# A hybrid Mamba-2 and short-convolution decoder layer on one core: y of four chunks kept in SBUF, a 128-row second product for the samples, and a new written order of the engines

## The chip, the cores and the metric

The kernel runs on one core of one Trainium2 chip. Its time is the device time of one execution in microseconds, as the median of several runs. The core has five engines that each take their own instructions in order: TensorE (PE; PEld is its weight load), VectorE (DVE), ScalarE (ACT), GpSimd (POOL) and SyncE (SP), which issues nearly all of the DMAs here. An engine whose next instruction waits for another engine or for a DMA holds everything that stands behind that instruction.

## What is computed

One decoder layer in float32 over a prompt of 1024 tokens, with 16 learned meta tokens ahead of it, and over 8 samples of 8 tokens that carry states. Cut to what matters here:

```python
proj = rmsnorm(h, norm_mix_pre) @ w_in         # gate_b, gate_c, hv, z, xbc, dt
u = gate_c * hv                                # short convolution, 512 wide
conv_u, new_buf_sc = causal_dwconv(u, buf_sc, sconv_w)
ya = group_rmsnorm(gate_b * conv_u, sconv_norm, 8)
xs, Bm, Cm = split(silu(causal_dwconv(xbc, buf_xbc, ssm_conv_w) + ssm_conv_b))
y, s = ssd_chunked(xs, dt, A, Bm, Cm, s, 128)  # 16 heads of 64, state 128
y = (y + D_skip * xs) * silu(z)
yb = group_rmsnorm(y, ssm_norm, 2)
h = h + rmsnorm(concat(ya, yb) @ w_out, norm_mix_post)
fn = rmsnorm(h, norm_ffn_pre)
h = h + rmsnorm((silu(fn @ w_gate) * (fn @ w_up)) @ w_down, norm_ffn_post)
```

The outputs are the rows of the prompt and of the samples and the new states of both convolutions and of the SSD recurrence.

## The kernel before

All products keep float32's accuracy by splitting an operand in a high and a low part of PE's faster type (fp32r): a projection is three products, high by high, high by low and low by high (`xh`, `xl` and `whi`, `wlo` in L398; `mhb`, `mlb` and `woh`, `wol` in L1192). The tokens are cut in chunks of 128, one to eight; 0 is the meta tokens and 9 the samples.

The work runs through these stages: the projections of x, B and C (`px`, to about 180 us); the projection of z (`pz`) and then the three of the short convolution (`pc`, `ph`, `pb`, each in groups 0 to 3 of 128 channels and token tiles 0 to 2, which are 256, 320 and 512 wide), to about 530 us, and among them the SSD passes of the chunks and the states of the samples; the output projection (`o`, three groups of chunks, L1192), to about 675 us; and the feed-forward part.

An SSD pass of chunk i (`ssd_chunk`, L859) makes y of the chunk (`y_of`, L702: the products `po` with the state and `pd` with the masked matrix M, L750, added on DVE up to L754) and the next state (`st`, L786; `S`, L873 and L875 on DVE). y_of stores y in the DRAM array d_y (L757). Later `finish(i)` (L759) loads it in a tile `yf` (two buffers, L761) and z in `zt`, multiplies (L766), forms the sums of squares (L768 to L772: `zt`, `sg`), takes them over the partitions by a product with ones (`pn`, L774), the root (L775) and the reciprocal (L776), scales (L779) and stores the result in d_yb (L780). FIN says after which chunk's pass which chunks are finished.

The short convolution's `sconv_out` (L836) multiplies a projection `pb` into `gc` (L840), squares it (L844), sums over groups by the product `sn` (L846), and takes the root (L847), the reciprocal (L850) and the product (L851); then the row goes to d_ya (L852).

A sample state (`sample_state`, L905; u from 0 to 7) takes the outer products of B and x of four samples by two products into one bank: `b1` holds B's high part in its upper and in its lower 64 rows, `xs2` the high part of x in rows 0 to 63 and the low part in rows 64 to 127, and so L938 gives high by high and high by low. `b2` holds B's low part in 64 rows, and L939 multiplies it by the upper 64 rows of xs2. Two such pairs make a state, and b1 and b2 are built on DVE for every second state.

Where the passes end, `final_state` (L972) transposes the last state S8 (`fsp`, L975), copies it on ACT (`fso`, L977) and stores it (L978). `slp` (L1010) and `slo` (L1012) do the same for the last rows of the convolution. The operands of the output projection come through `load_mix` (L1120): SP loads a chunk's finished rows (`mrb` from d_yb, L1126, two buffers; `mra` from d_ya), ACT makes the high part (`mhb`, L1133) and DVE the low one (`mlb`, L274). The weights come as `wo` (L1178), `woh` (ACT, L1181) and `wol` (DVE, L1182). A chunk's first four products need mhb, the fifth and sixth mlb.

The order of all this is not left to the program's text. ISSUE (L56) holds, for each of the five engines, the order of its instructions as numbered runs, and the code near L1620 puts each engine's instructions in that order.

Of the kernel before, what the change touches and what calls it, by code (L numbers as in the profile page):

```python
# [8 lines left out]
F32 = mybir.dt.float32  # L9
F32R = mybir.dt.float32r  # L10
# [6 lines left out]
P = 128  # L17
# [20 lines left out]
YB = 1  # L38
# [14 lines left out]
FIN = {4: (1,), 5: (2, 3, 4), 6: (5,), 7: (6,), 8: (7,), 9: (8,)}  # L53
# [179 lines left out]
def hymba_kernel(ctx, tc, x_prompt, x_sample, state_sconv, state_ssm_conv, state_ssm, meta_tokens,  # L233
# [647 lines left out]
    def samples_begin():  # L881
# [18 lines left out]
        E, y = y_of(i, xb, bt, xd, None)  # L900
        return xs2, bt, cs, E, y

    bms = {}

    def sample_state(u, st):  # L905

# [750 lines left out]
```

## Time and profile before

| | |
|---|---|
| median of three runs | 1387.33 us (1385.71, 1387.34, 1387.33) |
| the profiled execution | 1386.58 us |
| its span, first to last instruction | 1384.9 us |
| granted TensorE clock | 0.998 |
| DMA | 240.51 MB, mean 174 GB/s |

The page gives busy times of the engines over the span, a strip of 40 slices with tenths of busy time and of the granted clock, the chain of waits that ended last, and groups of instructions by line. A timeline's rows are start and duration in microseconds, the engine, the line, the operation, what it writes and reads, the shape and how many rows are taken together; a value in brackets is the time that the engine stood still ahead of it. PE's products overlap, so what a product costs PE is the distance to the next start. In a table of stretches the figures after the stretch's length are the busy times of PE, PEld, DVE, ACT and POOL, then the granted clock, the share of the DMA engines in use and GB/s. A row that begins with a line and ends in "| busy, mean" is a group of equal instructions.

### The profile page before, as it was taken

The numbers are of one execution on the slowest core, as the hardware profiler recorded it, in microseconds if no ns is written. First come the engines' busy times: TensorE is split into PE (matmuls) and PEld (weight loads), VectorE is DVE, ScalarE is ACT, GpSimd is POOL, SyncE is SP. The second block draws the span as 40 slices with busy tenths as digits, with TensorE's granted clock in tenths as the row PEclk, the third lists the DMA queues.
The fourth block names the chain that finished last, engine by engine and source line by source line (L and its number), as shares of the span: only waits on it lengthen the run. The fifth ranks groups of instructions, "written<-read, shape, count | busy, mean of one in ns | idle before, by whom it ended". The sixth has DMA issues, their size and how long they took to land.

```text
span 1384.9 us, 22044 instructions
## 1 busy us (share of the span) xinstructions
PE 1366.9 (99%) x8841; PEld 1228.5 (89%) x8841; DVE 976.9 (71%) x1332; ACT 585.9 (42%) x948; POOL 52.1 (4%) x106
## 2 busy tenths in 40 slices
PE   7999999999999999999999999999999999999997
PEld 6889998888898888887899999999999998888886
DVE  6555457878898988677599876766666766455565
ACT  6466445443364354556663233222232234344431
POOL 2000000000000000001100000000000000000001
PEclk9999999999999999999999999999999999999999
DMA  6136347778755457765445644344443379655543
GB/s 216 48 106 154 95 109 200 214 188 222 203 158 173 130 188 258 246 217 195 156 136 182 235 163 161 110 153 169 146 148 129 126 246 331 209 180 169 179 164 134
DMA packets 212543, 240.51 MB, mean 174 GB/s; under 512 B 33421, under 2 KB 161505, under 8 KB 212442
## 3 DMA queue, kind: packets, MB, share of 16 engines
q1 hardware_dynamic: 212442, 239.12, 54.6%
q8 instruction: 69, 1.13, 0.3%
q14 instruction: 32, 0.26, 0.1%
HBM read 170.29 MB, written 68.79 MB: 173 GB/s over the span
## 4 chain that ended last, share of the span: by engine, by line
PE 91%; DVE 4%; DMA 2%; ACT 1%; issue 1%; SPq 0%; POOL 0%; DVEq 0%; POOLq 0%; ACTq 0%
PE d L1580 15%; PE px L398 11%; PE o L1192 9%; PE pz L398 7%; PE yg L1237 6%; PE yu L1237 6%; PE xg L1237 4%; PE xu L1237 4%; PE zu L1237 4%; PE zg L1237 4%; PE pc L398 3%; PE pb L398 3%; PE ph L398 3%; PE pd L750 1%; PE st L786 1%
## 5 line engine op out<-in xcount | busy, mean ns | idle before, releaser
L398 PE MATMUL px<-xh,whi 128*128 128x272 f32 (+2 forms) x288 | 94.8, 337 | 0.0
L398 PE MATMUL px<-xl,whi 128*128 128x272 f32 (+2 forms) x288 | 93.7, 333 | 0.0
L398 PE MATMUL px<-xh,wlo 128*128 128x272 f32 (+2 forms) x288 | 93.3, 332 | 0.0
L274 DVE TENSOR_TENSOR wlo<-raw,whi 128x1024 fp32r<-128x1024 f32 x32 | 39.0, 1218 | 47.3 <-ACT whi L282 47.3
L1182 DVE SCALAR_TENSOR_TENSOR wol<-wo,vec,woh 128x1024 fp32r<-128x1024 f32 x36 | 46.0, 1279 | 34.7 <-ACT woh L1181 34.5
L398 PE MATMUL pz<-xh,whi 128*128 128x256 f32 (+2 forms) x192 | 64.6, 337 | 0.0
L1181 ACT ACTIVATE woh<-wo,vec 128x1024 fp32r<-128x1024 f32 x36 | 41.4, 1149 | 53.6 <-PE o L1192 42.5
L398 PE MATMUL pz<-xh,wlo 128*128 128x256 f32 (+2 forms) x192 | 63.9, 333 | 0.0
L398 PE MATMUL pz<-xl,whi 128*128 128x256 f32 (+2 forms) x192 | 63.7, 332 | 0.0
L430 DVE SCALAR_TENSOR_TENSOR xa<-xr,vec,xa 128x1128 f32<-128x1128 f32 x36 | 50.1, 1392 | 11.9 <-ACT xa L427 11.0
L398 PEld LDWEIGHTS px<-xh,whi 128*128 128x128 f32 x288 | 54.6, 193 | 4.3
L398 PEld LDWEIGHTS px<-xl,whi 128*128 128x128 f32 x288 | 54.0, 190 | 4.2 <-issue 0.2
L398 PEld LDWEIGHTS px<-xh,wlo 128*128 128x128 f32 x288 | 54.0, 190 | 3.7
L1580 PE MATMUL d<-wd,B01h 128*128 128x512 f32 x176 | 54.2, 389 | 0.0
L282 ACT ACTIVATE whi<-raw 128x1024 fp32r<-128x1024 f32 x32 | 33.8, 1055 | 38.4 <-PE px L398 18.2
L1580 PE MATMUL d<-wd,T3h 128*128 128x512 f32 x152 | 46.8, 389 | 0.0
L1192 PE MATMUL o<-wol,mhb 128*128 128x512 f32 x144 | 44.4, 394 | 0.0
L1580 PE MATMUL d<-wd,T2h 128*128 128x512 f32 x144 | 44.2, 389 | 0.0
L1580 PE MATMUL d<-wd,B11h 128*128 128x512 f32 x144 | 44.2, 389 | 0.0
L1192 PE MATMUL o<-woh,mhb 128*128 128x512 f32 x144 | 39.3, 397 | 1.3 <-ACT woh L1181 1.0
L1192 PE MATMUL o<-woh,mlb 128*128 128x512 f32 x128 | 40.3, 392 | 0.0
L398 PEld LDWEIGHTS pz<-xh,whi 128*128 128x128 f32 x192 | 36.1, 188 | 3.9 <-issue 1.3
(694 smaller groups left out, 4062.4 us busy)
## 6 DMA issues: line engine op xcount, KB each, us to landing
wo<-in_w_out_dram SPq DMA_DIRECT2D x36, 512.0 KB
raw<-in_w_in_dram SPq DMA_DIRECT2D x32, 512.0 KB
wg<-in_w_gate_dram SPq DMA_DIRECT2D x11, 1024.0 KB
wu<-in_w_up_dram SPq DMA_DIRECT2D x11, 1024.0 KB
xr<-in_w_down_dram SPq DMA_DIRECT2D x11, 1024.0 KB
d_t<-xr SPq DMA_DIRECT2D x11, 1024.0 KB
xt<-in_x_prompt_dram SPq DMA_DIRECT2D x16, 512.0 KB
M<-d_a SPq DMA_DIRECT2D x16, 512.0 KB
```

The source lines that it names most:

```text
L274: V.tensor_tensor(out=out, in0=a, in1=hi.bitcast(F32), op=ALU.subtract)
L282: S.activation(hi[:, :], raw[:, :], AF.Copy)
L398: PE.matmul(acc, (hi, lo, hi)[q][:, wk], (xh, xh, xl)[q][t][:, k, o:], start=n_ == 0, stop=n_ + 1 == len(order))
L430: V.scalar_tensor_tensor(out=dst, in0=part(row, i), scalar=wv[:, wcol(i):wcol(i) + 1], in1=dst, op0=ALU.mult, op1=ALU.add)
L750: PE.matmul(pdv[64 * e:64 * e + 64, h // 2, :w], xd[:w, h * 64:(h + 1) * 64], Ms[h // 8][:w, h % 8, :w], start=True, stop=True)
L786: PE.matmul(st[:, g * 512:(g + 1) * 512], bt[:w, g * P:(g + 1) * P], xw[:w, g * 512:(g + 1) * 512], start=True, stop=True)
L1181: S.activation(hi, raw, AF.Copy, scale=nv)
L1182: V.scalar_tensor_tensor(out=lo, in0=raw, scalar=nv, in1=hi[:, :].bitcast(F32), op0=ALU.mult, op1=ALU.subtract)
L1192: PE.matmul(accs[i][c], l[:, kb, :], r_[:, c * 512:(c + 1) * 512], start=n == 0 and q == 0, stop=n == 11 and q == len(steps) - 1)
L1237: PE.matmul(acc[:, c, 0:W1], w_[l][k], b[r_][:, k, c * W1:(c + 1) * W1], start=start and k == 0 and x == 0, stop=k == 3 and x == 2, skip_g ...
L1580: PE.matmul(accs[t], sx[x][:, tl], wx[y], start=st and x + y == 0, stop=en and x == 1, skip_group_check=n not in OPENS)
```

## The change

There are three parts.

First, y of chunks 4 to 7 stays in SBUF: the tile of y has two buffers instead of one (YB), y_of keeps it and finish works in it, so four stores to d_y and four loads from it go; yf of the other chunks has one buffer. FIN finishes chunks 4 to 7 each right after its own pass, and chunks 1, 2 and 3 after those of 5, 6 and 7.

Second, b2 becomes one tile of 128 rows for all states, whose lower 64 rows are filled with zeros once; L939 multiplies it by all 128 rows of xs2.

Third, ISSUE holds another order for all five engines. Of its numbers a first row stands for all.

```diff
-YB = 1
+YB = 2
+KEPT = (4, 5, 6, 7)
...
-FIN = {4: (1,), 5: (2, 3, 4), 6: (5,), 7: (6,), 8: (7,), 9: (8,)}
+FIN = {4: (4,), 5: (5, 1), 6: (6, 2), 7: (7, 3), 9: (8,)}
...
 ISSUE = {
     "Pool": """
-0+2 3+3 2+1 6+5 15+1 11+1 17+1 12+3 16+1 18+1 20+1 19+1 22+1 21+1 24+1 23+1 26+1 25+1 28+1 27+1 32+1 31+1 30+1 29+1
+0+2 3+3 2+1 6+4 15+1 10+2 17+1 12+3 16+1 18+1 20+1 19+1 22+1 21+1 24+1 23+1 26+1 25+1 28+1 27+1 32+1 31+1 30+1 29+1
...
-        SY.dma_start(d_y[i][:, :, :], y)
+        if i in KEPT:
+            kept[i] = y
+        else:
+            SY.dma_start(d_y[i][:, :, :], y)
+
+    kept = {}
...
-        y = pf.tile([P, 8, P], F32, tag="yf", name=f"yf{i}", bufs=2)
-        SY.dma_start(y[:, :, :w], d_y[i][:, :, :])
+        if i in KEPT:
+            y = kept.pop(i)
+        else:
+            y = pf.tile([P, 8, P], F32, tag="yf", name=f"yf{i}")
+            SY.dma_start(y[:, :, :w], d_y[i][:, :, :])
...
+        b2 = po.tile([P, 4, P], F32R, tag="bm2", name="bm2")
+        V.tensor_copy(b2[w:2 * w].rearrange("p a (c n) -> p (a c) n", n=w),
+                      ident[w:2 * w, 0:w].unsqueeze(1).to_broadcast([w, 8, w]))
+        bms["lo"] = b2
...
-            b2 = po.tile([w, 4, P], F32R, tag="bm2", name=f"bm2{u}")
+            b2 = bms["lo"]
...
-            for dst, h in ((b1[0:w], 0), (b1[w:2 * w], 0), (b2, w)):
+            for dst, h in ((b1[0:w], 0), (b1[w:2 * w], 0), (b2[0:w], w)):
...
-            PE.matmul(o, xs2[0:w, xj], b2[:, :, :].rearrange("p b n -> p (b n)"), start=False, stop=True)
+            PE.matmul(o, xs2[:, xj], b2[:, :, :].rearrange("p b n -> p (b n)"), start=False, stop=True)
```

The lines of the changed kernel are numbered otherwise: L1192 is L1203 there, L274, L398, L846, L850 and L851 are L273, L397, L853, L857 and L858, and L1126, L1133 and L1182 are L1137, L1144 and L1193. The numbers behind a name are those of the tiles; o_5181 and o_5195 are the first chunk's sums of the output projection in the new and the old order, mhb_5165 and mhb_5179 its high part, and d_yb_70 to d_yb_77 are chunks 1 to 8.

The order of PE where the state passes end and the output projection begins. Before, where the transposes `fsp` stand 76 rows ahead of the first o row, and pb and `sn` of the last group are still among the o products:

```order
L398 MATMUL pb_1_5056<-xl_170,whi 128x320
L1192 MATMUL o_5195<-woh_5201,mhb_5179 128x512 x2
L1192 MATMUL o_5195<-wol_5202,mhb_5179 128x512 x2
L1192 MATMUL o_5196<-woh_5201,mhb_5185 128x512 x2
L398 MATMUL pb_2_5089<-xh_168,whi 128x512
L398 MATMUL pb_2_5089<-xh_168,wlo 128x512
L398 MATMUL pb_2_5089<-xl_171,whi 128x512
L846 MATMUL sn_5050<-sq_5048,bd_125 128x256
```

Now, with `pd` and `st` of chunk 8 a few rows ahead:

```order
L397 MATMUL pb_2_5075<-xh_168,wlo 128x512
L397 MATMUL pb_2_5075<-xl_171,whi 128x512
L986 MATMUL fsp<-ident,S_4800 128x128 x8
L853 MATMUL sn_5102<-sq_5034,bd_125 128x512
L1021 MATMUL slp<-ident,slast 18x128 x4
L781 MATMUL pn_5284<-sg_5281,ones 128x2x64
L1203 MATMUL o_5181<-woh_5187,mhb_5165 128x512 x2
L1203 MATMUL o_5181<-wol_5188,mhb_5165 128x512 x2
L1203 MATMUL o_5181<-woh_5187,mlb_5166 128x512 x2
L1203 MATMUL o_5181<-woh_5211,mhb_5165 128x512 x2
L1203 MATMUL o_5181<-wol_5212,mhb_5165 128x512 x2
```

All products of pb, which stood between fsp and the o products and among these, now stand ahead of fsp.

The order of DVE at the same place. Before, a piece from the reciprocals of the convolution's third row on (`sq_4944`) with the first two low parts mlb, which the o products read:

```order
L850 RECIPROCAL sq_4944<-sq_4944 128x256
L840 TENSOR_TENSOR gc_4220<-pb_2_4983,gc_4220 128x512
L1182 SCALAR_TENSOR_TENSOR wol_5202<-wo_5199,vec,woh_5201 128x1024
L850 RECIPROCAL sq_4944<-sq_4944 128x320
L274 TENSOR_TENSOR mlb_5180<-mrb_5177,mhb_5179 128x1024
L840 TENSOR_TENSOR gc_4618<-pb_0_5022,gc_4618 128x256
L274 TENSOR_TENSOR mlb_5186<-mrb_5183,mhb_5185 128x1024
```

Now, the row that ends the state's update (S_4800, for which fsp waits) and those behind it, and then the end of the same list with the first two low parts:

```order
L882 TENSOR_TENSOR S_4800<-st_4797,S_4800 128x1024
L847 TENSOR_TENSOR gc_4620<-pb_2_5075,gc_4620 128x512
L778 TENSOR_TENSOR zt_5277<-zt_5277 128x2x2x64
L779 TENSOR_TENSOR sg_5281<-zt_5277 128x2x64
L1193 SCALAR_TENSOR_TENSOR wol_5212<-wo_5209,vec,woh_5211 128x1024
L857 RECIPROCAL sq_5034<-sq_5034 128x160 x2
L857 RECIPROCAL sq_5034<-sq_5034 128x256
```

```order
L857 RECIPROCAL sq_4930<-sq_4930 128x256
L858 TENSOR_TENSOR gc_4209<-gc_4209,sq_4930 128x512
L858 TENSOR_TENSOR gc_4209<-gc_4209,sq_4930 128x320
L858 TENSOR_TENSOR gc_4209<-gc_4209,sq_4930 128x256
L1023 COPY slo<-slp 18x512
L273 TENSOR_TENSOR mlb_5166<-mrb_5163,mhb_5165 128x1024
L273 TENSOR_TENSOR mlb_5172<-mrb_5169,mhb_5171 128x1024
```

Between the two pieces stand the reciprocal of sg (L783), two products yf (L786), a reciprocal of sq_5034 with 256 columns and three products L858 of gc_4620. The reciprocals and products of the convolution's last two rows, gc_4209 and gc_4620, which stood among the low parts or behind them, now stand between the state's update and the first low part.

The order of SP there. Before:

```order
L757 DMA d_y_87<-y_4725 128x1024
L978 DMA out_dram<-fso 128x8x128
L1126 DMA mrb_5177<-d_yb_70 128x1024
L1126 DMA mrb_5183<-d_yb_71 128x1024
L780 DMA d_yb_76<-yf_4801 128x1024
L764 DMA zt_5420<-d_z 128x8x128
L1178 DMA wo_5305<-in_w_out_dram 128x1024
L762 DMA yf_5418<-d_y_87 128x1024
L1126 DMA mrb_5189<-d_yb_72 128x1024
L1126 DMA mrb_5377<-d_yb_73 128x1024
L1126 DMA mrb_5383<-d_yb_74 128x1024
```

Now, from the last load of zt on:

```order
L771 DMA zt_5406<-d_z 128x8x128
L1189 DMA wo_5315<-in_w_out_dram 128x1024
L989 DMA out_dram<-fso 128x8x128
L1137 DMA mrb_5163<-d_yb_70 128x1024
L1137 DMA mrb_5169<-d_yb_71 128x1024
L1088 DMA xt_5621<-in_x_prompt_dram 128x1024
L1048 DMA post_bc<-in_norm_mix_post_dram 128x1024
L1088 DMA xt_5677<-in_x_prompt_dram 128x1024
L1050 DMA ffn_bc<-in_norm_ffn_pre_dram 128x1024
```

```order
L859 DMA d_ya<-gc_4209 128x1088
L1024 DMA out_dram<-slo 16x512
L1025 DMA out_dram<-slo 2x512
L1137 DMA mrb_5175<-d_yb_72 128x1024
L1137 DMA mrb_5363<-d_yb_73 128x1024
L769 DMA yf_5404<-d_y_87 128x1024
```

The store of fso stands ahead of the first two loads mrb in both orders. Between the second and the third mrb stood four transfers; now it is nine, with the stores of two of the convolution's rows (d_ya) and of slo among them.

More of the change, by code (lines that the diff above doesn't have):

```diff
@@ L879, in hymba_kernel @@
     o_nat = o_s_s[0].rearrange("b g e p n -> b (g e p) n")
+    bms = {}
     def samples_begin():
@@ L901, in samples_begin @@
         return xs2, bt, cs, E, y
-    bms = {}
     def sample_state(u, st):
```

296 rows, old and new, of the table ISSUE are left out of this document.

## The prediction

> **What bounds the kernel now.** I read the page first, then the table of stretches for the two stages in which the change does most, and then single rows.
>
> ```profile
> span 1384.9 us, 22044 instructions
> PE 1366.9 (99%) x8841; PEld 1228.5 (89%) x8841; DVE 976.9 (71%) x1332; ACT 585.9 (42%) x948; POOL 52.1 (4%) x106
> PEclk9999999999999999999999999999999999999999
> PE 91%; DVE 4%; DMA 2%; ACT 1%; issue 1%; SPq 0%; POOL 0%; DVEq 0%; POOLq 0%; ACTq 0%
> 330.00:520.00 190.00, 190.00 (x1297) 165.38 (x1296) 168.11 (x217) 90.10 (x160) 6.18 (x10) 1.00 0.61 176
> 520.00:675.00 155.00, 153.73 (x699) 125.11 (x698) 112.82 (x127) 84.33 (x118) 11.88 (x12) 1.00 0.70 227
> ```
>
> PE is busy 99% of the span, and the chain of waits runs 91% over PE. So two things alone move the time: PE's own work, and new moments at which PE stands. In 330 to 520 us (first figure after the length: PE) PE has no gap at all, while DVE (third figure) is busy 168 of 190 us; in the output projection (520 to 675 us) PE lacks 1.3 us. There is almost nothing to win from waits, and much to lose if PE's order runs into DVE's.
>
> The executions shown have a median of 1387.33 us. The profiled one took 1386.58 us, 1.7 us more than its span; I sum against 1386.58, which lies 0.75 us below the median.
>
> **Part 1: the second product over 128 rows.** The start times in PE's timeline around the first sample state:
>
> ```profile
> 240.29 0.31 PE L398 MATMUL pz<-xl,whi 128*128 128x320 f32 x1
> 240.44 0.40 PE L938 MATMUL s1p<-bm,xs 128*128 128x512 f32 x1
> 240.76 0.49 PE L939 MATMUL s1p<-bm,xs 64*128 64x512 f32 x1
> ...
> 242.05 0.42 PE L398 MATMUL pz<-xh,whi 128*128 128x320 f32 x1
> 242.30 0.31 PE L398 MATMUL pz<-xh,wlo 128*128 128x320 f32 x1
> ...
> 244.36 0.39 PE L398 MATMUL pz<-xh,whi 128*128 128x512 f32 x1
> 244.59 0.40 PE L398 MATMUL pz<-xh,wlo 128*128 128x512 f32 x1
> L939 PE MATMUL s1p<-bm,xs x16: 492/498/502, 240.8 to 442.8; 64*128 64x512 f32 x16
> ```
>
> The second column is a product's duration; what PE pays is the distance from one start to the next. With 128 rows a 512-wide one takes 244.59 - 244.36 = 0.23 us, and a 320-wide one 240.44 - 240.29 = 0.15. The four products of a state, alternating between 128 and 64 rows, take 242.05 - 240.44 = 1.61 us, and the next product 0.25 instead of 0.15. With 128 rows throughout I expect 4 x 0.23 + 0.15 = 1.07 instead of 1.86 us: 0.79 us per state, and 16 products at L939 are 8 states, so **6.3 us less**. The bounds: nothing (if the 64-row form is not what costs), and 16 x (0.498 - 0.23) = 4.3 us plus 8 x 0.5 us for L938's share of the alternation, 8.3. I take 6.3, which these rows give directly. The copy of zeros that fills the tile's lower half once is one DVE instruction more; a small one here costs 0.3 us, and in 187 to 330 us PE never waited.
>
> [...]
>
> In the new order the products with M (L750, 64 columns of output) of chunks 6 and 8 stand in one run each instead of two. At 0.1 us for entering and 0.1 for leaving such a run (0.25 against 0.15 above) that is **0.4 us less**.
>
> **Part 2: y kept in SBUF.** Four stores and four loads of 512 KB go. In 330 to 520 us PE had no gap, so no load of y held it, and the queue's share (0.61, the last figure but one of that row) leaves room: I cost it at nothing, and no gain is possible where nothing waited. It moves the finishing of chunks 1 to 3 to the end, and so the load of DVE.
>
> **Part 3: the order at the handover** from the state passes to the output projection. Before, after the transposes of the final state:
>
> ```profile
> 506.29 1.04 PE L975 MATMUL fsp<-ident,S 128*128 128x128 f32 x8
> 520.87 0.63 PE L1192 MATMUL o<-woh,mhb 128*128 128x512 f32 x2
> 507.39 1.01 ACT L977 ACTIVATE fso<-fsp 128x1024 f32<-128x1024 f32 x1
> 508.43 0.39 SPq L978 DMA_DIRECT2D out_dram<-fso  x1
> 508.87 1.76 SPq L1126 DMA_DIRECT2D mrb<-d_yb  x2
> 519.15 8.29 SPq L1126 DMA_DIRECT2D mrb<-d_yb  x3
> L1133 ACTq EVENT_SEMAPHORE  x1: 17/17/17, 514.8 to 514.8; - x1
> L1133 ACT ACTIVATE mhb<-mrb x4: 1047/1050/1062, 515.5 to 525.1; 128x1024 fp32r<-128x1024 f32 x4
> 523.95 2.20 ACT L1133 ACTIVATE mhb<-mrb 128x1024 fp32r<-128x1024 f32 x2
> 530.75 1.53 PE L1192 MATMUL o<-woh,mhb 128*128 128x512 f32 x6
> 532.12 0.39 PE L1192 MATMUL o<-wol,mhb 128*128 128x512 f32 x1
> 532.81 1.02 PE L846 MATMUL sn<-sq,bd 128*128 128x512 f32 x2
> 533.67 0.60 PE L1010 MATMUL slp<-ident,slast 128*18 128x128 f32 x4
> 534.03 0.71 PE L1192 MATMUL o<-wol,mhb 128*128 128x512 f32 x2
> ```
>
> From fsp's end (507.3) to the first o product lay 13.5 us of pb products, and under them went fso (ACT), its store, the load of mrb1 (issued 508.87, landed by 514.8: 5.9 us) and mhb1. SP stays in order: mrb1 stands behind the store of fso, before and after. After the change the pb products all stand ahead of fsp, and between fsp and the first o product are only sn32, slp and pn9.
>
> What PE has from the end of S8 (DVE, L875, for which fsp waits) until the fifth o product, the first to read mlb1: fsp 1.0, sn32 and slp 534.03 - 532.81 = 1.2, pn9 0.3 (my estimate, as the shorter of two such small products), four o products at (532.12 - 530.75) / 6 = 0.23, 0.9: together 3.4 us. DVE's list over the same stretch is priced by its groups in 504 to 550 us (name, shape, busy time, mean ns):
>
> ```profile
> L1182 DVE SCALAR_TENSOR_TENSOR wol<-wo,vec,woh 128x1024 fp32r<-128x1024 f32 x6 | 7.6, 1262 | 0.2
> L850 DVE RECIPROCAL sq<-sq 128x256 f32<-128x256 f32 x3 | 5.1, 1728 | 0.0
> L274 DVE TENSOR_TENSOR mlb<-mrb,mhb 128x1024 fp32r<-128x1024 f32 x4 | 4.8, 1199 | 0.0
> L850 DVE RECIPROCAL sq<-sq 128x160 f32<-128x160 f32 x2 | 2.2, 1120 | 0.0
> L776 DVE RECIPROCAL sg<-sg 128x128 f32<-128x128 f32 x1 | 0.9, 944 | 0.0
> L851 DVE TENSOR_TENSOR gc<-gc,sq 128x512 f32<-128x512 f32 x2 | 1.4, 687 | 0.0
> 512.50 1.74 DVE L850 RECIPROCAL sq<-sq 128x256 f32<-128x256 f32 x1
> 514.16 0.63 DVE L840 TENSOR_TENSOR gc<-pb,gc 128x512 f32<-128x512 f32 x1
> ```
>
> Between S8 and mlb1 now stand one wol (1.26), reciprocals of 2 x 160, 3 x 256 and 128 columns (2.24 + 5.18 + 0.94) and twelve light ones, the longest 687 ns, half a microsecond in the mean (6.0); with mlb1 itself (1.20) that is 16.8 us. A row starts 0.08 us ahead of the end of the one before (512.50 + 1.74 against 514.16), so 20 rows take 1.6 us less: **mlb1 is ready 15.2 us after S8**. PE then stands 15.2 - 3.4 = **11.8 us** in two pieces: first for mhb1, which is ready after fsp 1.0, fso 1.0, an issue 0.4, the load 5.9 and mhb1 1.05, that is 9.4 us after S8, where PE has 2.5 us of work (6.9 us); then for mlb1 (15.2 - 9.4 - 0.9: 4.9 us). Behind the waiting product stands all of the output projection, so nothing of PE's passes it.
>
> A third piece: mrb3 takes mrb1's buffer, so SP issues it only when mlb1 is done, and holds yf8 and the next loads behind it (before: issued 519.15, mhb3 begun 523.95, 4.8 us). mhb3 is ready 4.8 + 1.05 = 5.9 us after mlb1, and PE has 20 products, 4.6 us, so it waits **1.3 us**. Bounds of part 3: 11 us, if DVE is 5% quicker and mrb3 lands within PE's 4.6 us; 19 us, if each load takes twice as long (mhb1 5.9 us later, which swallows the wait for mlb1 but for 0.3, and mhb3 4.8 later). I take 13.1, the nearest to these rows.
>
> Is it given back? PE lacked 1.3 us in the whole projection, so at most that much of a later wait can be absorbed, and after 675 us PE is full.
>
> **Part 4: the rest of the order.** I find one more place, pb of group 2, tile 1, whose bank DVE frees only behind a reciprocal of chunk 7 (256 columns, some 1.73 us), and a few of half a microsecond. DVE, at 168 of 190 us, has 22 us to spare, but spread. I allow **2.5 us**, between 0 and 5.
>
> **Sum**: 1386.6 - 6.3 - 0.4 + 11.8 + 1.3 + 2.5 = 1395.5; I forecast **1395.5 us**, 0.6% slower.
>
> **Rivals.**
>
> *The 64-row cost stays* (the products are as slow at 128 rows, since it is their operands and not their rows that slow them): 1395.5 + 6.3 = 1401.8. Against it: L398's and L1192's products of 128 rows next to one another start 0.23 us apart. 8%.
>
> *PE is slow after standing still.* The start of the trace shows one program line at two rates:
>
> ```profile
> 15.91 1.11 PE L398 MATMUL px<-xh,whi 128*128 128x272 f32 x4
> 20.26 1.16 PE L398 MATMUL px<-xh,wlo 128*128 128x272 f32 x8
> ```
>
> Four take 1.11 us, and 4.3 us later eight 1.16: half the rate at first, though the granted clock reads 9 throughout. If the rate drops again in the 6.9 us of standing, the first four o products go from 0.9 to 1.8 us under the wait for mlb1, and the 20 behind it from 4.6 to at most 9.2; of that, 1.3 us replace the wait for mhb3. That is 2.1 - 1.3 = 0.8 us more if half the rate lasts 4.3 us as between these rows, 3.3 more if it lasts through all 20: 1396.3 to 1398.8. 22%.
>
> [...]
>
> *The loads bunch* at the handover (fso's store, y8, two mrb and two xt are in one queue, already at a share of 0.61): landing twice as late costs 19 instead of 13 us, 1401.5. 10%.
>
> *The handover is covered* (this one is not slower): DVE's list would have to be through before PE reaches o. It decides at 3.4 us after S8: if the reciprocals and products of gc2 and gc3 ran ahead of S8, mlb1 would follow mhb1 directly, and only the wait for mhb1 would stay: 1386.6 - 6.7 + 6.9 is 1386.8, with the other small waits 1387 to 1390, no change (6%). If mrb1's load were also issued ahead of fso's store, nothing is left of part 3: 1386.6 - 6.7 + 2.5 = 1382.4 (5%). Against both: the two engines run in the order written, where S8 stands ahead of that list and the store ahead of the load.
>
> *y isn't kept in effect*, or to no end: with no wait of PE on its loads, that gives the same sum.
>
> **How the numbers follow.** Forecast 49%, the rivals 8, 22, 10 and 6 + 5%. The range runs from the sum with part 3 at its 11 us and part 4 at nothing (1390.9), and a little of the covered case, up to the slow ends: 1389 to 1402. A change of 0.2% (2.8 us) is about what a measurement of this kernel can tell: faster 0.05, same 0.06, slower 0.89, by these cases.
>
> **What would show it.** L939 at 0.39 us and the four products of a state at 0.9 (part 1); two waits of PE on mhb1 and mlb1 of 7 and 5 us next to each other, and a 1 us wait on mhb3 (part 3); the list of PE's waits would name mhb and mlb, in the order of 13 us together. If those waits are absent the forecast is wrong in sign; if L939 stays at 0.5 it is too low.

## The result, and the profile after

| | before | after |
|---|---|---|
| median of 6 runs each | 1386.86 us (1385.71 to 1387.34) | 1396.35 us (1395.93 to 1398.17) |
| the profiled execution | 1386.58 us | 1395.93 us |
| DMA | 240.51 MB | 236.32 MB |

The ratio is 1.0073, with a 95% interval of 1.0063 to 1.0083: the changed kernel is 9.5 us slower, and transfers 4.2 MB less.

The span and the clock's strip from the changed kernel's page:

```profile
span 1394.0 us, 22043 instructions
...
PEclk9999999999999998999999999999999999999999
```

Its two stretches as in the prediction (start and end, length, busy time of PE, PEld, DVE, ACT and POOL, granted clock, DMA share, GB/s):

```profile
330.00:520.00 190.00, 189.44 (x1293) 167.02 (x1291) 166.58 (x212) 83.25 (x143) 3.54 (x10) 1.00 0.49 142
520.00:675.00 155.00, 142.28 (x625) 113.44 (x625) 108.15 (x124) 82.27 (x113) 11.90 (x12) 0.96 0.68 227
```

Up to 520 us PE still has practically no gap (0.6 us in 190). From 520 us on it lacks 12.7 us where it lacked 1.3, and the granted clock, 1.00 before, reads 0.96. One slice of the clock's strip shows an 8. So the whole loss is to be looked for behind 520 us. The list of PE's waits (in total, times, longest) has new entries near its top:

```profile
PE o L1203 <- ACT mhb L1144: 8.6, 2, 7.9
PE pre L359 <- DMA pre_row<-in_norm_mix_pre_dram: 2.3, 1, 2.3
...
PE o L1203 <- DVE mlb L273: 1.6, 1, 1.6
```

The two on mhb and mlb are new; the one on pre, at the start of the kernel, was there before with 2.4 us. PE's timeline at that place:

```profile
520.06 1.09 PE L986 MATMUL fsp<-ident,S 128*128 128x128 f32 x8
521.79 1.12 PE L853 MATMUL sn<-sq,bd 128*128 128x512 f32 x2 [0.64 <-ACT sq L851]
...
523.70 0.49 PE L781 MATMUL pn<-sg,ones 128*128 128x128 f32 x2 [0.34 <-ACT sq L854]
532.04 1.22 PE L1203 MATMUL o<-woh,mhb 128*128 128x512 f32 x2 [7.86 <-ACT mhb L1144]
...
535.75 1.22 PE L1203 MATMUL o<-woh,mlb 128*128 128x512 f32 x2 [1.63 <-DVE mlb L273]
536.76 1.05 PE L1203 MATMUL o<-woh,mhb 128*128 128x512 f32 x2
537.62 1.05 PE L1203 MATMUL o<-wol,mhb 128*128 128x512 f32 x2
...
541.41 0.62 PE L1203 MATMUL o<-woh,mhb 128*128 128x512 f32 x2
541.87 0.62 PE L1203 MATMUL o<-wol,mhb 128*128 128x512 f32 x2
...
543.68 0.73 PE L1203 MATMUL o<-woh,mhb 128*128 128x512 f32 x2 [0.74 <-ACT mhb L1144]
```

and the stretch's busy times and clock:

```profile
530.00:540.00 10.00, 6.33 (x14) 4.54 (x15) 6.83 (x10) 2.11 (x2) 0.00 (x0) 0.50 1.05 404
```

In brackets stand the idle time and who ended it: 0.64, 0.34, 7.86, 1.63 and 0.74, together **11.2 us**. The second thing is the distance of the rows: two products start 0.86 us after the two before them at 537 us (537.62 - 536.76), and 0.46 us at 541.9. PE runs at half rate behind its long wait, and this time the stretch's clock says so: 0.50. Between 532.04 and 543.68 stand 24 products, which took 11.64 - 1.63 - 0.74 = 9.3 us instead of 24 x 0.23 = 5.5: another **3.7 us**. Together 14.9 us. (Whether the 3.7 would have been waited for otherwise, the rows alone don't say.)

The other engines there (the same timeline of SP's queue, ACT and DVE):

```profile
523.07 0.39 SPq L989 DMA_DIRECT2D out_dram<-fso  x1
523.51 2.54 SPq L1137 DMA_DIRECT2D mrb<-d_yb  x2
530.94 1.06 ACT L1144 ACTIVATE mhb<-mrb 128x1024 fp32r<-128x1024 f32 x1 [6.34 <-DMA mrb<-d_yb]
518.84 1.16 DVE L882 TENSOR_TENSOR S<-st,S 128x1024 f32<-128x1024 f32 x1
534.49 2.34 DVE L273 TENSOR_TENSOR mlb<-mrb,mhb 128x1024 fp32r<-128x1024 f32 x2
535.61 0.91 SPq L1025 DMA_DIRECT2D out_dram<-slo  x1
536.61 1.14 SPq L1137 DMA_DIRECT2D mrb<-d_yb  x2
542.57 1.06 ACT L1144 ACTIVATE mhb<-mrb 128x1024 fp32r<-128x1024 f32 x1 [9.28 <-DMA mrb<-d_yb]
```

S8 ends at 520.0. mhb1 is ready at 532.0, 12.0 us later; the first of the two mlb is ready at about 535.7, 15.7 us later. Only then is mrb3 issued (536.61), and mhb3 begins 6.0 us after that. The last 0.8 us ahead of this issue are not mlb1's: SP, in its own order, was still at the second store of slo until 536.5.

### The profile page after: what moved, and what is told of

Read it like the earlier page. It is cut to its first block, busy times and chain, and to the rows that moved or that the text cites. A ratio compares the mean times of both kernels' runs of the same rounds, so it can differ in the third digit from the quotient of the medians.

```text
span 1394.0 us, 22043 instructions
## 1 busy us (share of the span) xinstructions
PE 1364.7 (98%) x8841; PEld 1229.0 (88%) x8841; DVE 979.1 (70%) x1333; ACT 586.7 (42%) x948; POOL 48.2 (3%) x106
## 2 busy tenths in 40 slices
DMA packets 211391, 236.32 MB, mean 170 GB/s; under 512 B 33293, under 2 KB 161377, under 8 KB 211290
## 4 chain that ended last, share of the span: by engine, by line
PE 88%; DVE 2%; ACT 1%; DMA 1%; issue 1%; SPq 0%; POOL 0%; DVEq 0%; POOLq 0%; ACTq 0%
PE d L1591 15%; PE o L1203 9%; PE px L397 8%; PE yu L1248 7%; PE yg L1248 7%; PE pz L397 7%; PE zu L1248 5%; PE zg L1248 5%; PE xg L1248 4%; PE xu L1248 4%; PE pc L397 3%; PE pb L397 3%; PE ph L397 3%; PE pd L749 1%; PE st L793 1%
## 5 line engine op out<-in xcount | busy, mean ns | idle before, releaser
L397 PE MATMUL px<-xh,whi 128*128 128x272 f32 (+2 forms) x288 | 94.1, 335 | 0.1
L397 PE MATMUL px<-xl,whi 128*128 128x272 f32 (+2 forms) x288 | 93.0, 330 | 0.0
L397 PE MATMUL px<-xh,wlo 128*128 128x272 f32 (+2 forms) x288 | 92.6, 329 | 0.0
L273 DVE TENSOR_TENSOR wlo<-raw,whi 128x1024 fp32r<-128x1024 f32 x32 | 39.0, 1218 | 48.6 <-ACT whi L281 48.5
L1193 DVE SCALAR_TENSOR_TENSOR wol<-wo,vec,woh 128x1024 fp32r<-128x1024 f32 x36 | 46.2, 1282 | 37.8 <-ACT woh L1192 37.8
L397 PE MATMUL pz<-xh,whi 128*128 128x256 f32 (+2 forms) x192 | 64.5, 336 | 0.3 <-DVE z L812 0.3
L397 PE MATMUL pz<-xh,wlo 128*128 128x256 f32 (+2 forms) x192 | 63.8, 332 | 0.0
L397 PE MATMUL pz<-xl,whi 128*128 128x256 f32 (+2 forms) x192 | 63.6, 331 | 0.0
L1192 ACT ACTIVATE woh<-wo,vec 128x1024 fp32r<-128x1024 f32 x36 | 41.4, 1149 | 49.5 <-PE o L1203 43.2
L429 DVE SCALAR_TENSOR_TENSOR xa<-xr,vec,xa 128x1128 f32<-128x1128 f32 x36 | 50.1, 1392 | 12.3 <-ACT xa L426 10.2
L397 PEld LDWEIGHTS px<-xh,whi 128*128 128x128 f32 x288 | 53.7, 190 | 4.6 <-ACT xr L458 0.3
L397 PEld LDWEIGHTS px<-xl,whi 128*128 128x128 f32 x288 | 53.3, 188 | 4.2 <-issue 0.2
L397 PEld LDWEIGHTS px<-xh,wlo 128*128 128x128 f32 x288 | 53.3, 188 | 3.7
L1203 PE MATMUL o<-woh,mhb 128*128 128x512 f32 x144 | 41.1, 409 | 9.9 <-ACT mhb L1144 8.6
L1203 PE MATMUL o<-wol,mhb 128*128 128x512 f32 x144 | 45.3, 402 | 0.2 <-DVE wol L1193 0.2
L1203 PE MATMUL o<-woh,mlb 128*128 128x512 f32 x128 | 41.0, 400 | 1.7 <-DVE mlb L273 1.6
L1203 PEld LDWEIGHTS o<-woh,mhb 128*128 128x128 f32 x144 | 27.0, 193 | 17.2 <-ACT mhb L1144 9.2
```

What stands on the lines that cost most here:

```text
L273: V.tensor_tensor(out=out, in0=a, in1=hi.bitcast(F32), op=ALU.subtract)
L397: PE.matmul(acc, (hi, lo, hi)[q][:, wk], (xh, xh, xl)[q][t][:, k, o:], start=n_ == 0, stop=n_ + 1 == len(order))
L429: V.scalar_tensor_tensor(out=dst, in0=part(row, i), scalar=wv[:, wcol(i):wcol(i) + 1], in1=dst, op0=ALU.mult, op1=ALU.add)
L1192: S.activation(hi, raw, AF.Copy, scale=nv)
L1193: V.scalar_tensor_tensor(out=lo, in0=raw, scalar=nv, in1=hi[:, :].bitcast(F32), op0=ALU.mult, op1=ALU.subtract)
L1203: PE.matmul(accs[i][c], l[:, kb, :], r_[:, c * 512:(c + 1) * 512], start=n == 0 and q == 0, stop=n == 11 and q == len(steps) - 1)
```

## The experiments

Three readings of the loss were to be told apart. **A**: DVE's list between S8 and the low parts sets when PE goes on. **Loads**: mrb1 behind the store of fso sets it. **C**: the half rate after the standstill is lost on top. Beside them stood the two small parts, the 128 rows and y in SBUF. All the kernels were timed in three rounds or more beside the kernel before, whose median was 1386.8 to 1387.2 us in these jobs. The last column is taken from the one profiled execution of each kernel: from the first product of the first sample state (`s1p`) to the end of the span. It leaves out what lies ahead of that state, where executions in one and the same order differ by up to 2.7 us (the last section says more on this); differences of 1 or 2 us are better read from it than from the medians.

| run | median, us | ratio to before, 95% | first sample state to end, us |
|---|---|---|---|
| before | 1386.86 | | 1144.4 |
| changed | 1396.35 | 1.0073 [1.0063, 1.0083] | 1155.3 |
| rows 64 again | 1402.02 | 1.0112 [1.0097, 1.0127] | 1159.7 |
| kernel before, 128 rows alone | 1381.44 | 0.9959 [0.9945, 0.9974] | 1139.7 |
| loads early | 1396.83 | 1.0072 [1.0055, 1.0088] | 1154.3 |
| PE kept busy | 1398.64 | 1.0083 [1.0068, 1.0098] | 1156.1 |
| loads and low parts early | 1396.58 | 1.0067 [1.0050, 1.0084] | 1154.3 |
| y of chunk 4 through DRAM | 1397.77 | 1.0080 [1.0065, 1.0095] | 1155.0 |
| mrb3 ahead of xt | 1399.96 | 1.0094 [1.0077, 1.0111] | 1156.3 |
| the list behind | 1391.60 | 1.0038 [1.0025, 1.0050] | 1149.3 |

### The second product over 64 rows again

```diff
-            PE.matmul(o, xs2[:, xj], b2[:, :, :].rearrange("p b n -> p (b n)"), start=False, stop=True)
+            PE.matmul(o, xs2[0:w, xj], b2[0:w, :, :].rearrange("p b n -> p (b n)"), start=False, stop=True)
```

> The changed kernel with the samples' second product over 64 rows again (the order and everything else as changed). My theory, that the alternation of 128-row and 64-row products costs 0.79 us in each of 8 states: 6.3 us slower than the changed kernel (1396.35), 1402.7, with the four products of a state at 1.6 us from the first start to the next other product instead of 0.94. The rival, that the rows of a product don't matter and the gain came with the new order: 1396 and no change in those distances.

1402.02 us, 5.7 more than the changed kernel. The group of the second product (shortest, median and longest in ns), in this run and then in the changed kernel:

```profile
L950 PE MATMUL s1p<-bm,xs x16: 491/500/502, 240.4 to 437.0; 64*128 64x512 f32 x16
```

```profile
L950 PE MATMUL s1p<-bm,xs x16: 388/395/398, 238.9 to 431.0; 128*128 128x512 f32 x16
```

The first state in PE's timeline, in this run:

```profile
240.12 0.40 PE L949 MATMUL s1p<-bm,xs 128*128 128x512 f32 x1
240.44 0.49 PE L950 MATMUL s1p<-bm,xs 64*128 64x512 f32 x1
...
241.73 0.42 PE L397 MATMUL pz<-xh,whi 128*128 128x320 f32 x1
241.99 0.31 PE L397 MATMUL pz<-xh,wlo 128*128 128x320 f32 x1
```

and in the changed kernel:

```profile
238.65 0.40 PE L949 MATMUL s1p<-bm,xs 128*128 128x512 f32 x1
...
239.59 0.31 PE L397 MATMUL pz<-xh,whi 128*128 128x320 f32 x1
239.73 0.31 PE L397 MATMUL pz<-xh,wlo 128*128 128x320 f32 x1
```

Four products take 1.61 us with 64 rows in the second and 0.94 with 128, and the product behind them 0.26 and 0.14: 0.79 us per state, as forecast. The eight states would make 6.3. From the first sample state to the end the two traces differ by 4.4 us, so some of the 5.7 between the medians lies ahead of the first state and is no gain of the rows. Product beside product, the eight states gain 6.1 us (about 0.79 in six of them, 0.70 in two); 1.3 us of that is given back between the states by 440 us (0.3 of it in a wait of PE for DVE, pz, that the changed kernel has and this run has not), and 0.4 us behind 520 us. The rest of what is given back was not traced to a cause.

### The kernel before with the 128-row product alone

The order, y and everything else as before; one instruction, the zeros, comes in.

```diff
+        b2 = po.tile([P, 4, P], F32R, tag="bm2", name="bm2")
...
-            PE.matmul(o, xs2[0:w, xj], b2[:, :, :].rearrange("p b n -> p (b n)"), start=False, stop=True)
+            PE.matmul(o, xs2[:, xj], b2[:, :, :].rearrange("p b n -> p (b n)"), start=False, stop=True)
```

> The kernel before with the 128-row second product alone (the zeros are one more VectorE instruction; y through DRAM and the old order otherwise). My theory: 6.3 us less than before (1386.86), 1380.6, since no wait of the handover is brought in. The rival, that the gain of the product is swallowed by waits of the old order: between 1383 and 1387. If 1380.6, the whole loss of the change lies in the new order.

1381.44 us: 5.35 less than before, and the fastest of all kernels here. From the first sample state to the end it is 4.8 us less, so the 128 rows are worth about the same in both orders (4.4 in the new one). What the change adds beside them, the new order with y kept, costs 1396.35 - 1381.44 = **14.9 us** by the medians and 1155.3 - 1139.7 = 15.6 by the traces. The waits and the half rate gave 14.9; that the medians give the same to a tenth is chance, but the size is confirmed.

### The loads early

The first two loads mrb are issued right behind the last store of y and ahead of the store of fso (whose tile comes from another pool for it). The numbers are those of SP's instructions: the first then stands ahead of the second.

```diff
+MOVE = {'SP': [(214, 234), (215, 234)]}
```

> The changed kernel with the loads mrb1 and mrb2 issued right behind the store of y8 instead of behind the store of fso (fso's tile moves to another pool, so that this is possible); VectorE's order is as changed. Theory A, that VectorE's list ahead of mlb1 sets the end: mhb1 is there 5 to 6 us earlier, the first four o products too, but mlb1 comes no earlier (15 us after S8), so PE stands for mlb1 instead of mhb1 and the time stays within 1 us of 1396.35. Theory B, that the load behind fso's store sets it: 5 to 6 us less, 1391.

1396.83 us, no gain (1.0 us from the first sample state to the end). PE's waits in this run:

```profile
PE o L1204 <- DVE mlb L274: 8.7, 1, 8.7
...
PE o L1204 <- ACT mhb L1145: 1.4, 1, 1.4
```

The wait for mhb falls from 7.9 to 1.4 us, and the one for mlb grows from 1.6 to 8.7. Without the delay of mrb1 the end stays where it is: the load was only the first of two conditions. This is A, and the reading by loads falls.

### PE kept busy

Thirty-four products more, of one weight tile by itself, into the bank of the second group ahead of that group's own first product, which overwrites them: 8 us of work in the place of the standstill.

```diff
+                if n == 0 and i == 1:
+                    for _ in range(34):
+                        PE.matmul(accs[i][0], hi[:, 0:P], hi[:, 0:512], start=True, stop=True)
```

> The changed kernel with 34 more products (woh by woh, into the bank that the first o product then overwrites) between pn9 and the first o product, where PE stands still for 7.9 us: they fill about that time and keep PE at its rate. The next o products should then start 0.23 us apart instead of 0.43. Theory A, that mhb3 (behind mlb1 and mrb3) sets the time at which the third chunk's products start: PE is through the 24 products 3 to 4 us earlier and waits the longer for mhb3, and the time stays within 0.6 us of 1396.35. Theory C, that the half rate is a loss of its own: 3.6 us less, 1392.7.

1398.64 us, 2.3 more than the changed kernel, where A expected it within 0.6. PE's timeline:

```profile
522.03 1.09 PE L987 MATMUL fsp<-ident,S 128*128 128x128 f32 x8
...
525.92 8.00 PE L1204 MATMUL o<-woh 128*128 128x512 f32 x34
533.87 0.73 PE L1207 MATMUL o<-woh,mhb 128*128 128x512 f32 x2
534.45 0.62 PE L1207 MATMUL o<-wol,mhb 128*128 128x512 f32 x2
537.72 0.74 PE L1207 MATMUL o<-woh,mlb 128*128 128x512 f32 x2 [2.65 <-DVE mlb L274]
...
539.30 1.05 PE L1207 MATMUL o<-woh,mlb 128*128 128x512 f32 x2
540.15 1.05 PE L1207 MATMUL o<-woh,mhb 128*128 128x512 f32 x2
...
545.78 0.73 PE L1207 MATMUL o<-woh,mhb 128*128 128x512 f32 x2 [1.60 <-ACT mhb L1145]
```

The first four products now take 1.2 us (537.72 - 2.65 - 533.87) instead of 2.1, and the twenty behind them 6.5 instead of 7.2, since PE fell to half the rate again (540.15 - 539.30 = 0.85 for two). So the run takes away 1.6 of the 3.7 us of half rate, and PE waits 1.0 us longer for mlb and 0.9 longer for mhb3. From fsp to the first product of the third chunk (the last row) it is 545.78 - 522.03 = 23.75 us, in the changed kernel 543.68 - 520.06 = 23.62. What was taken away had lain under the waits for mlb and mhb3, so it cost nothing up to there: A again, not C. (The half rate that was left is not tested by this run; but what ends ahead of mhb3 is the load of mrb3, which needs nothing that the o products make.) Of the 2.7 us between the two profiled executions (1398.64 and 1395.93), 2.0 lie ahead of the first sample state (240.63 against 238.65 us), where the two kernels are the same, and 0.6 behind the output projection, where no cause was traced.

### Loads and low parts early

As the loads early; besides, mlb1 and mlb2 stand ahead of the reciprocal for sg, and mrb3 and mrb4 ahead of the stores of yf and of the convolution's rows.

```diff
+MOVE = {'SP': [(214, 234), (215, 234), (216, 225), (229, 225)], 'DVE': [(547, 559), (548, 559)]}
```

> As the run with the early loads (mrb1 and mrb2 behind the store of y8, 1396.83), and also mlb1 and mlb2 on VectorE ahead of the reciprocal of sg9, behind 4.5 instead of 15 us of its list, and mrb3 and mrb4 ahead of the stores of yf9 and the convolution's rows. Theory A, that VectorE's list ahead of mlb1 is what PE waits for: mlb1 about 7 to 8 us earlier, two waits of PE of 1 and 2.5 us instead of 8 to 9 and 1.4, the o products at the full rate, and 8 to 9 us less than that run: 1388, about the time of the kernel before. The rival, that the rest of VectorE's list, now later, is waited for further on: 1391 or more, with a new wait of PE in the output projection.

1396.58 us, where 1388 was expected: a miss. The timeline's rows of PE, SP, ACT and DVE in this run:

```profile
529.79 1.22 PE L1204 MATMUL o<-woh,mlb 128*128 128x512 f32 x2 [0.63 <-DVE mlb L274]
540.36 1.22 PE L1204 MATMUL o<-woh,mhb 128*128 128x512 f32 x2 [4.24 <-ACT mhb L1145]
529.76 1.46 SPq L1138 DMA_DIRECT2D mrb<-d_yb  x2
539.25 1.06 ACT L1145 ACTIVATE mhb<-mrb 128x1024 fp32r<-128x1024 f32 x1 [10.41 <-DMA mrb<-d_yb]
542.84 0.08 DVE L1058 MEMSET shift<- 128x24 f32 x1 [3.66 <-DMA d_ya<-gc]
```

The wait for mlb1 shrinks to 0.6 us, and the next conditions stand behind it. mrb3 now follows directly on the loads of xt, post_bc, xt and ffn_bc (2 MB together), and mhb3 begins 9.5 us after its issue instead of 6.0; PE waits 4.2 us for it, at half rate behind; and mlb3 stands on DVE behind a memset that waits for a store of the convolution's rows.

### Y of chunk 4 through DRAM again

```diff
-KEPT = (4, 5, 6, 7)
+KEPT = (5, 6, 7)
```

> The changed kernel with y of chunk 4 through DRAM again (one store and one load of 512 KB more, the store right when y4 is done, the load ahead of zt4's; yf1 is loaded later, since the one buffer of yf is used by chunk 4 first). My step, that keeping y takes away nothing that PE waits for: 1396.35 within 1 us. The rival, that each round trip costs PE (4 of them, and 4 MB): 2 us or more from this one.

1397.77 us. From the first sample state to the first product `d` it is 1158.6 - 240.5 = 918.1 us, in the changed kernel 1157.0 - 238.7 = 918.3, so the round trip of this chunk costs nothing. The median lies 1.4 us above that of the changed kernel, between the 1 us of the one expectation and the 2 us of the rival; in these two traces 1.8 us lie ahead of the first sample state, where nothing was changed. The other three chunks were not tried.

### mrb3 ahead of xt

As the one before the last; mrb3 and mrb4 stand ahead of the loads of xt, and mlb3 ahead of the memset.

```diff
+MOVE = {'SP': [(214, 234), (215, 234), (216, 246), (229, 246)], 'DVE': [(547, 559), (548, 559), (549, 546)]}
```

> As the run with the early loads and low parts (1396.58), with mrb3 and mrb4 issued ahead of the four loads xt, post_bc, xt, ffn_bc (2 MB) instead of behind them, and mlb3 on VectorE ahead of the memset of shift. Theory D, that with the list out of the way the load of mrb3 sets the end, since it shares the DMA engines with those 2 MB (9.5 us from issue to landing, against 5.9 before the change), and PE then goes at half its rate a second time: mrb3 lands in 5 to 6 us, the wait for mhb3 falls from 4.2 to about 1 us, that for mlb3 from 1.7 to nothing, the products behind go at the full rate, and the time is 7 to 9 us less: 1388.5. Theory A alone (VectorE's list was all): it was wrong with 1396.58 already. The rival, that what is issued later is waited for later: 1393 or more.

1399.96 us, where 1388.5 was expected: a miss again, 3.6 us slower than the changed kernel (1.0 from the first sample state to the end). PE's waits in this run:

```profile
PE o L1204 <- DVE wol L1194: 5.4, 1, 5.4
PE o L1204 <- DVE mlb L274: 3.9, 2, 3.3
```

mhb3 comes in time now, and PE waits for the next things in DVE's list: 3.3 us for mlb3, which still stands behind the convolution's reciprocals and slo, and 5.4 us for a wol behind the memset. It is the same list, further on.

### The list behind

So more of the list was put behind what PE reads first: mlb3 ahead of a reciprocal of the convolution, two wol ahead of slo and the memset, and on ACT one woh ahead of a square.

```diff
+MOVE = {'SP': [(214, 234), (215, 234), (216, 246), (229, 246)], 'DVE': [(547, 559), (548, 559), (549, 524), (555, 545), (562, 546)], 'Activation': [(442, 449)]}
```

> As the run with mrb3 ahead of xt (1399.96), whose waits moved on to mlb3 (3.3 us, behind the end of VectorE's list) and to wol6 (5.4 us, behind the memset of shift and yf8, which wait for a store and a load). Now mlb3 stands ahead of the last reciprocal of gc2, wol6 ahead of slo, wol7 ahead of the memset, and on ScalarE woh7 ahead of the square of yf8. Theory E, that the loss is VectorE's order throughout, work that waits for DMAs or that nobody needs yet ahead of what the next o products need: both waits go but for 0.5 us, with them two stretches at half the rate (3.5 us): 10 to 11 us less, 1389 to 1390, 2 to 3 us above the kernel before. The rival, that VectorE has too much work there whatever its order, so that each move only shifts the wait: 1396 or more, with a wait of 4 us or more at a later weight.

1391.60 us (6 runs), 4.75 less than the changed kernel (6.0 from the first sample state to the end), where 1389 to 1390 was expected. PE's timeline:

```profile
527.58 0.73 PE L1204 MATMUL o<-woh,mhb 128*128 128x512 f32 x2 [1.40 <-ACT mhb L1145]
...
529.42 1.22 PE L1204 MATMUL o<-woh,mlb 128*128 128x512 f32 x2 [0.65 <-DVE mlb L274]
...
550.28 0.70 PE L782 MATMUL pn<-sg,ones 128*128 128x256 f32 x2 [2.14 <-DVE sg L780]
```

and a stretch of it with its clock:

```profile
529.00:535.00 6.00, 5.58 (x13) 4.43 (x14) 5.93 (x9) 1.44 (x2) 0.00 (x0) 0.50 0.97 321
```

The long waits are gone, and with them about a third of the loss, so A is shown from its other side. What PE lost, it does not get back whole: 2.1 us are waited for the next thing that DVE put off (sg), and six microseconds run at half rate with no long wait ahead of them. The kernel is still 10.2 us behind the old order with 128 rows (9.6 from the first sample state to the end). The waits from 520 us on make 5.3 of these (2.1, 1.4, 0.7, 0.6, 0.3 and 0.2) and the half rate about 2.9 (14 products in 6.1 us instead of 3.2); the rest was not traced. The opposite step, the pb products back between fsp and the first o product with nothing else changed, was not tried, so how much of the loss that alone would take away stays open.

## Why the prediction was right

1395.5 us was forecast and 1396.35 measured, and the new waits stand where it put them. Its terms, one by one:

- **Part 1, -6.3**: too large. The medians give -5.35 in the old order and -5.7 in the new one, the traces from the first sample state to the end -4.8 and -4.4. The price of a state was right (about 0.79 us in six of eight); what it left out is that some of this is given back afterwards, 0.3 us of it in a new wait for DVE (pz). A 64-row product between 128-row ones measures 500 ns (the run with 64 rows again), a 128-row one in its place 395 (the changed kernel). The rival by which the cost stays fell with the same rows.
- **The runs of M, -0.4**: not measured by itself. The rows of before agree with the 0.1 us at each end of such a run: 0.21 us from the last pb product to it (495.65 - 495.44) and 0.22 from the first one behind it to the next (496.89 - 496.67), where pb products of that width otherwise start 0.12 apart.
- **Part 2, 0**: right for chunk 4, the one that was tried.
- **Part 3, 6.9 + 4.9 for mhb1 and mlb1**: the time of mlb1 was right (15.7 us after S8, forecast 15.2). mhb1 came 12.0 us after S8 instead of 9.4: its load was issued 3.5 us after S8 instead of 2.4, and took 7.4 us until ACT's start instead of 5.9. So the two waits are split otherwise, 7.86 (with 0.64 and 0.34 ahead of it) and 1.63, and their end is the same: where one engine's list sets the time, the split does not matter.
- **mhb3, +1.3**: 0.74 of waiting, with 2.6 us more under it, since the 20 products ahead took 7.2 us instead of 4.6. mhb3 was ready 7.9 us after mlb1, forecast 5.9: the load took 6.0 us instead of 4.8, and mrb3 was issued 0.9 us after mlb1's end, because SP was still at the stores of slo. That SP's own list also stands ahead of this load, the prediction left out. This term was mis-sized: with the half rate on the first four products (1.2 us) the handover costs 14.9 us instead of 13.1.
- **Part 4, +2.5**: too large. Up to 520 us one wait of 0.4 us is new beside the one on pz (pb, for DVE's u).
- **Given back, at most 1.3**: 0.9 us. The wait of yg for u2g in the FFN's first stretch is not in the list of after.

So part 3 was 1.8 us too small and part 1's gain 1.5 to 1.9 too large, and against that stand part 4, 2.1 too large, and the 0.9 given back. That the sum was right to 1 us is luck in part. From the first sample state to the end the changed kernel is 10.9 us slower (1155.3 against 1144.4), where the sum had 8.9; the terms above place 0.3 to 0.7 of these 2.0 us, and the rest is open. In the profiled executions this is made up ahead of that state, which the changed kernel reached 1.8 us earlier (238.65 against 240.44), as no experiment with the same order did. What is right without luck is the mechanism of part 3: which waits come, where, and which list sets their end.

Of the rivals, *PE is slow after standing still* did happen, with half the rate from 532.0 to 540.9 us, where the prediction gave it 22%. That it costs little on top was right, for the reason given there: the lost time lies under the waits for mlb1 and mhb3. The kernel kept busy shows that for 1.6 of the 3.7 us; there the waits grew by what the rate gave. In the changed kernel the half rate came behind a wait of 7.9 us and lasted 8.9 us, with the 1.6 us wait for mlb1 in it, and still 5.2 us behind that wait; in two of the experiments it came after waits that were all shorter (2.65 us; 1.40 and 0.65).

*The loads bunch* did not set the end here, but a later load did hold PE in the run with the loads and low parts early (mrb3, 9.5 instead of 6.0 us). *The handover is covered* was rightly small, and its two conditions were too few: with the loads early and the first two low parts ahead of most of the list, much as it asked, the time did not move, because mrb3 on SP, and on DVE the memset, mlb3, two wol and sg, came one after another as the next condition.

## What to carry to other kernels

Where an engine has 15 us of instructions in order between a result and the operand that another engine reads next, that other engine needs 15 us of work of its own there; moving that work (here 13 us of products) away costs what it covered (here 11.2 us of waits), with hardly an instruction added. Ahead of moving one entry of such a list, price the whole list against the reader's needs: each entry freed here, up to the last run, only named the next. And a change of several parts should be timed in parts: here one of them is worth about 5 us alone, and the package loses 9.5.

## What was not expected of the hardware

- **Half rate after short waits.** With PE busy for 8.0 us and then waiting 2.65, the products 1.6 us later ran at 0.43 us each for 3.3 us; with the list behind, waits of 0.65, 0.34, 1.40 and 0.65 us within 6 us were followed by 6 us at a granted clock of 0.50. What triggers it was not settled.
- **A spell of half clock with no wait at all**, at 61 to 64 us. The kernel before and the changed one, the same stretch:

```profile
61.00:64.00 3.00, 3.00 (x15) 3.00 (x14) 1.25 (x6) 2.96 (x5) 0.43 (x2) 0.50 0.23 90
```

```profile
61.00:64.00 3.00, 3.00 (x25) 3.00 (x24) 0.93 (x6) 2.97 (x5) 0.00 (x0) 1.00 0.44 170
```

PE is busy throughout in both (3.00 of 3.00); in the first it does 15 products, in the second 25. All the experiments' profiles show the spell too, with clocks of 0.50 to 0.78. In the seven experiments whose order up to there is that of the changed kernel (all but the old order) the first sample state comes at 240.1 to 241.4 us, in the changed kernel's profile at 238.7. In three of them, 64 rows again, loads early and kept busy, PE's product ptv, ahead of the spell, comes at 42.4, 42.4 and 42.9 us instead of 42.1; the other 1.2 us of their distance arise between it and the first sample state, a stretch with the spell in it. So distances within a trace are better evidence here than medians 2 us apart. Only one execution of each kernel was profiled, so how many of the others had the spell is not known.
